# Query, key, silu-gate and merge-gate projections of a two-branch layer as Strassen pairs, with kept operand sums and one branch's products spilled

## The chip, the cores and the metric

One Trainium2 chip, one core. The metric is the device time of one execution in microseconds (us). Before the change three runs gave a median of 2404.2 us (2403.67 to 2405.09). Every product is made in 4-byte numbers split in two parts (below), on TensorE (PE); VectorE is DVE, ScalarE is ACT, GpSimd is POOL, and SyncE (SP) issues the weight loads.

## The reference

Two layers over 512 frames of width 1024. A layer is an RMSNorm, one wide projection, two recurrent branches, a gated merge, a feed-forward block and a gated embedding:

```python
h = rmsnorm(x, norm1_g[i]);  z = h @ w_in[i] + b_in[i]
_, _, mv, mo, mi, mf, rq, rk, rv, rg, gm, gr = split_cols(z)
...                                        # branch A: mLSTM, 4 heads, y_m = sigmoid(mo) * headnorm(hm)
rq4 = rope(rq...);  rk4 = rope(rk...) * (R_DK ** -0.5)
hr = retention_chunkwise(rq4, rk4, rv, log_gamma)          # 4 heads, 256 wide q and k, 512 wide v
y_r = silu(rg) * head_layernorm(hr, r_norm_g[i], R_HEADS)
merged = sigmoid(gm) * (y_m @ w_bm[i]) + sigmoid(gr) * (y_r @ w_br[i])
x = x + merged @ w_out[i]
h2 = rmsnorm(x, norm2_g[i])
x = x + square(relu(h2 @ w_ff1[i] + b_ff1[i])) @ w_ff2[i] + b_ff2[i]
x = x + sigmoid(rmsnorm(x, norm3_g[i]) @ w_pe_gate[i]) * (p[i] @ w_pe[i])
```

## The kernel before, in words

Activations stand transposed, 8 tiles of 128 features by 512 frames. **Each operand is a pair of high and low parts**: `split` (L238) makes the high part by an ACT copy into the rounded type, and the low part by a DVE subtraction (L240). `mm3` (L313) multiplies high by high, high by low and low by high, so one product costs three matmuls. The norm's factor per frame (`n1.b`) is multiplied in after the product, since the projection runs on `x` times the gain (`xa`).

The program is **a list of units** (`unit_list`, L110), in the order in which PE takes them. A `T8` unit is one weight block of 1024 by 128 (512 KB): 24 matmuls of 512 columns into one PSUM bank (`t8`, L318). A `V` unit is a quarter of a value projection, 24 matmuls as well. A `PAIR` unit, used by the second feed-forward product (`ff2`) alone, makes two output tiles over 1024 of the 4096 inner columns by Strassen's scheme in Winograd's form: 7 products of 12 matmuls of 256 columns, 84 in all, in the order P1, (P4 of the pair before), P5, P2, P6, P3, P7. Three PSUM banks serve a pair: P1, P6, P7 and P4 accumulate in bank a, P2 in b, P5 and P3 in c, and after most of the products DVE reads the bank before the next one adds to it. A pair's weights are four blocks and four sums of blocks, in pieces A, B, C (128 by 1024) and D (128 by 512).

Weights flow through **three stages**: `fill_raws` (L276) loads raw pieces on SP's queue into 5 buffers; `prep_next` (L289) splits the next piece, ACT then DVE, into one of 3 buffers (`PIECES`); PE uses it. `ready` (L300) places the split of piece n+2 ahead of unit n's matmuls (`LOOK`), so a split is issued when the buffer of three pieces earlier has been used.

The sums of blocks (t1 to t4) are made in DRAM by POOL: `sum_steps` (L251) copies 1 MB and adds 1 MB with accumulating DMAs, 8 steps for each of the 8 groups of four pairs. `unit` (L304) issues one slot of this list at every third unit; each step waits for the matmul that stood last, as a pace.

A layer's stages, one after the other: 4 mLSTM heads (query and key with a convolution, whose 3 border columns POOL copies at L689; scores, whose diagonal POOL masks at L736; `attend`; output gate `m_out`), with the merge gate A (`gate_tile`, L813) in between, kept in `mA`; retention head 0's query and key (`r_qk`, L767: product times norm, z, at L775, then the rotation at L781 to L783, then a split); the first branch's output product, multiplied into `mA` (L870 to L872); values, scores, `attend` and the gates (`r_out`, L803) of the retention heads; the second branch's product and gate B (L900 to L913); `w_out`; the feed-forward block; the embedding gate. Short-lived tiles come from `tmp`, a ring of 7 tiles of 128 by 512. Cosine and sine lie in tiles of their own. `decay`, `br_spill` and the residual `xr` are loaded on ACT's queue.

An engine takes its instructions in the order in which they stand in its queue; where one waits, all behind it wait.

Of the kernel before, what the change touches and what calls it, by code (L numbers as in the profile page):

```python
# [53 lines left out]
RAWS = 5  # L54
# [40 lines left out]
STEP = 3  # L95


def pair_schedule(n):

    out = []  # L100
    for i in range(n):
        out.append((i, "P1"))
        if i:
            out.append((i - 1, "P4"))
        out += [(i, x) for x in ("P5", "P2", "P6", "P3", "P7")]
    out.append((n - 1, "P4"))
    return out


def unit_list(i):  # L110
# [9 lines left out]

    def mqk(h):
# [9 lines left out]
    def rqk(h):  # L131
        for d in range(2):
            t8("w_in", CRQ + h * 256 + d * P)
        for d in range(2):
            t8("w_in", CRK + h * 256 + d * P)

    def rg(h):
        for d in range(4):
            t8("w_in", CRG + h * 512 + d * P)
# [15 lines left out]
    full("w_in", CGM, 0, 2, 8)  # L155
    mo(3)
    rqk(0)
    full("w_bm")
# [12 lines left out]
    for c in range(8):  # L171
        t8("w_in", CGR + c * P)
        t8("w_br", c * P, 1024)
    full("w_out")
    def pairs(seq):
        for kind, b, p in seq:
            if kind == "f":
                t8("w_ff1", b * 1024 + 256 * p)
                t8("w_ff1", b * 1024 + 256 * p + P)
            else:  # L180
                u.append(("PAIR", i, b, p))
# [9 lines left out]
def build(ctx, tc, ins, out):  # L191
# [27 lines left out]
    br_dram = tc.dram_tile([L, KT, P, T], F32, name="br_spill")  # L219

# [4 lines left out]
    ones = cpool.tile([P, P], F32, name="ones")  # L225
    gp.memset(ones, 1.0)
    ones_r = cpool.tile([P, P], F32R, name="ones_r")
    ve.tensor_copy(ones_r, ones)
# [14 lines left out]
    sums = {(i, b, x): tc.dram_tile([4, P, Q], F32, name=f"s{i}{b}{x}") for i in range(L) for b in range(4) for x in MADE}  # L243

    def block(i, b, x):
        return ins["wpairs"][i, b, GIVEN.index(x)] if x in GIVEN else sums[i, b, x]
# [4 lines left out]
    def sum_steps(i):  # L251

        def copy(b, x):
            return gp.dma_start(flat(block(i, b, x)), flat(block(i, b, MADE[x][0])), max_dma_last_dim=4096)

        def add(b, x):
            return gp.dma_start(flat(block(i, b, x)), flat(block(i, b, MADE[x][1])), accum_op=OP.add,
                                max_dma_last_dim=4096)

        def step(f, b, x):  # L260

            if f:
                tc.add_manual_dep(f(b, x).ins, cur["mm"].ins.name, SYNC, reason="pace of the sums")

        for b in range(4):
            for f, x in ((copy, "t1"), (copy, "t3"), (add, "t1"), (add, "t3"), (copy, "t2"), (None, None), (add, "t2"),
                         (None, None), (copy, "t4"), (None, None), (add, "t4")):
                yield lambda f=f, b=b, x=x: step(f, b, x)
# [5 lines left out]
    at = {"unit": 0, "prep": 0, "load": 0, "whole": 0}  # L274

    def fill_raws(most=RAWS):  # L276
        while at["load"] < len(order) and len(raws) < most:
            n, x = order[at["load"]]
            raws[n, x] = r = wpool.tile([P, UN], F32, name=f"wr{at['load']}", tag="wr", bufs=RAWS)
            if x:  # L280
                _, i, b, p = units[n]
                for k, y in enumerate(PIECE[x]):
                    nc.sync.dma_start(r[:, k * Q:(k + 1) * Q], block(i, b, y)[p])
# [5 lines left out]
    def prep_next():  # L289
# [5 lines left out]
        pl = cur["xw"] if x == "D" else cur["last"] if n >= NU - LAST else wpool  # L295
        out_ = [pl.tile([P, w], F32R, name=f"w{a}{n}_{x}", tag=f"{'d' if x == 'D' else 'w'}{a}") for a in "hl"]
# [7 lines left out]
    def unit(kind):  # L304
        n = at["unit"]
        at["unit"] += 1
        if n % STEP == 0 and "mm" in cur:
            next(cur["steps"], lambda: None)()
# [9 lines left out]
    def t8(act, name):  # L318
# [16 lines left out]
    class Pair:  # L335


        def __init__(self, name, n, act, done):
            self.name, self.n, self.act, self.done = name, n, act, done
            self.bank = {}  # L340

        def product(self, x):
            w, half, j = PRODUCTS[x]
            ready(place[self.n, "A"] + READY[x])
            wh, wl = [a[:, half * Q:(half + 1) * Q] for a in pieces[self.n, w]]
            b = {"P2": "b", "P5": "c", "P3": "c"}.get(x, "a")
            first = x in ("P1", "P2", "P5")
            if first:
                self.bank[b] = ps(f"{self.name}{b}")
            o = self.bank[b][:, 0:S]  # L350
            m = slice(j * S, (j + 1) * S)
            for k in range(4):
                s = slice(k * P, (k + 1) * P)
                h, l = self.act[k]
                f, e = first and k == 0, k == 3
                te.matmul(o, wh[:, s], h[:, m], start=f, stop=False, skip_group_check=True)
                te.matmul(o, wh[:, s], l[:, m], start=False, stop=False, skip_group_check=True)  # L357
                te.matmul(o, wl[:, s], h[:, m], start=False, stop=e, skip_group_check=True)
            self.done(x, o)

    def run_pairs(make):

        n = at["unit"]
        at["unit"] += len(make)
        live = {}
        for i, x in pair_schedule(len(make)):
            if i not in live:
                live[i] = make[i](n + i)
            live[i].product(x)
            if x == "P4":  # L370
# [853 lines left out]
```

## Time and profile before

| | |
|---|---|
| median of 3 runs | 2404.2 us |
| the profiled execution | 2404.53 us |
| its span (first to last instruction) | 2402.8 us |
| granted TensorE clock, mean | 0.996 |
| PE busy, matmuls | 2381.9 us (99%), 12212 |
| DVE busy | 1500.7 us (62%) |
| ACT busy | 1051.8 us (44%) |
| POOL busy | 178.9 us (7%) |
| moved by DMA | 333.72 MB, 139 GB/s |

"Busy" counts from an instruction's start to its end, and matmuls overlap; what one matmul costs PE is the distance between two starts. A group's row gives its count, busy time, mean duration and the idle time of its engine just before it with what ended that. A wait row gives the microseconds an engine stood still, how often and the longest. A DMA row gives the size of one and the median time from issue to landing.

### The profile page before, as it was taken

The numbers are of one execution on the slowest core, as the hardware profiler recorded it, in microseconds if no ns is written. First come the engines' busy times: TensorE is split into PE (matmuls) and PEld (weight loads), VectorE is DVE, ScalarE is ACT, GpSimd is POOL, SyncE is SP. The second block draws the span as 40 slices with busy tenths as digits, with TensorE's granted clock in tenths as the row PEclk, the third lists the DMA queues.
The fourth block names the chain that finished last, engine by engine and source line by source line (L and its number), as shares of the span: only waits on it lengthen the run. The fifth ranks groups of instructions, "written<-read, shape, count | busy, mean of one in ns | idle before, by whom it ended". The sixth has DMA issues, their size and how long they took to land.

```text
span 2402.8 us, 31079 instructions
## 1 busy us (share of the span) xinstructions
PE 2381.9 (99%) x12212; PEld 2036.4 (85%) x12212; DVE 1500.7 (62%) x2276; ACT 1051.8 (44%) x1434; POOL 178.9 (7%) x266
## 2 busy tenths in 40 slices
PE   9999999999999999999999999999999999999997
PEld 8888888888888898899888888888888888998996
DVE  6867536654555576677778665466625556676675
ACT  5746323332333445445557552233323335445453
POOL 3101000000000100000201100000000010000012
PEclk9999999999999999999999999999999999999998
DMA  6433453545365553444444445344454654443451
GB/s 229 134 103 110 146 149 105 150 127 167 113 169 165 151 158 117 141 154 132 147 142 125 127 119 163 118 123 133 122 167 136 175 167 123 154 146 116 140 161 36
DMA packets 114883, 333.72 MB, mean 139 GB/s; under 512 B 11689, under 2 KB 14121, under 8 KB 114737
## 3 DMA queue, kind: packets, MB, share of 16 engines
q1 hardware_dynamic: 87392, 246.66, 31.2%
q0 software_dynamic: 17408, 67.11, 11.8%
q10 hardware_dynamic: 9936, 17.96, 2.4%
q8 instruction: 96, 1.57, 0.3%
q14 instruction: 51, 0.41, 0.1%
HBM read 323.30 MB, written 75.50 MB: 166 GB/s over the span
## 4 chain that ended last, share of the span: by engine, by line
PE 97%; DVE 1%; issue 1%; DMA 1%; POOL 0%; ACT 0%; SPq 0%; POOLq 0%; DVEq 0%; ACTq 0%
PE l0f L314 2%; PE l1f L314 2%; PE l1f L316 2%; PE l1f L315 2%; PE l0f L316 2%; PE l0f L315 2%; PE l1br L315 1%; PE l1br L314 1%; PE l0br L314 1%; PE l0br L316 1%; PE l0br L315 1%; PE l1br L316 1%; PE l0bgm L314 1%; PE l1bgm L314 1%; PE l0pg L314 1%; PE l0pg L315 1%
## 5 line engine op out<-in xcount | busy, mean ns | idle before, releaser
L239 ACT ACTIVATE wh<-wr 128x1024 fp32r<-128x1024 f32 x342 | 362.0, 1059 | 836.2 <-issue 161.7
L240 DVE TENSOR_TENSOR wl<-wr,wh 128x1024 fp32r<-128x1024 f32 x342 | 418.4, 1224 | 220.5 <-ACT wh L239 220.0
L314 PE MATMUL l0f<-l0n2h,wh 128*128 128x512 f32 x256 | 99.8, 390 | 0.0
L314 PE MATMUL l1f<-l1n2h,wh 128*128 128x512 f32 x256 | 99.8, 390 | 0.0
L316 PE MATMUL l1f<-l1n2h,wl 128*128 128x512 f32 x256 | 99.7, 389 | 0.0
L316 PE MATMUL l0f<-l0n2h,wl 128*128 128x512 f32 x256 | 99.7, 389 | 0.0
L315 PE MATMUL l1f<-l1n2l,wh 128*128 128x512 f32 x256 | 99.6, 389 | 0.0
L315 PE MATMUL l0f<-l0n2l,wh 128*128 128x512 f32 x256 | 99.6, 389 | 0.0
L239 ACT ACTIVATE wh_C<-wr 128x1024 fp32r<-128x1024 f32 x32 | 33.9, 1060 | 67.4 <-PE l0f L315 5.6
L316 PEld LDWEIGHTS l0f<-l0n2h,wl 128*128 128x128 f32 x256 | 48.1, 188 | 10.2
L316 PEld LDWEIGHTS l1f<-l1n2h,wl 128*128 128x128 f32 x256 | 48.0, 188 | 10.1
L314 PEld LDWEIGHTS l1f<-l1n2h,wh 128*128 128x128 f32 x256 | 48.1, 188 | 9.8
L315 PEld LDWEIGHTS l1f<-l1n2l,wh 128*128 128x128 f32 x256 | 48.1, 188 | 9.8
L315 PEld LDWEIGHTS l0f<-l0n2l,wh 128*128 128x128 f32 x256 | 48.1, 188 | 9.7
L314 PEld LDWEIGHTS l0f<-l0n2h,wh 128*128 128x128 f32 x256 | 48.1, 188 | 9.7
L240 DVE TENSOR_TENSOR wl_C<-wr,wh_C 128x1024 fp32r<-128x1024 f32 x32 | 39.2, 1226 | 18.3 <-ACT wh_C L239 17.9
L239 ACT ACTIVATE wh_A<-wr 128x1024 fp32r<-128x1024 f32 x32 | 33.8, 1056 | 30.5 <-PE l1f L315 9.8
L240 DVE TENSOR_TENSOR wl_A<-wr,wh_A 128x1024 fp32r<-128x1024 f32 x32 | 40.4, 1264 | 10.3 <-ACT wh_A L239 9.4
L239 ACT ACTIVATE wh_B<-wr 128x1024 fp32r<-128x1024 f32 x32 | 33.7, 1053 | 27.1 <-PE l0o02a L357 1.8
L240 DVE TENSOR_TENSOR wl_B<-wr,wh_B 128x1024 fp32r<-128x1024 f32 x32 | 39.1, 1221 | 7.9 <-ACT wh_B L239 7.9
L239 ACT ACTIVATE wh_D<-wr 128x512 fp32r<-128x512 f32 x32 | 20.1, 628 | 37.1 <-PE l0o01a L357 1.8
L429 POOL TENSOR_TENSOR l1n3sum<-l1n3sum,l1n3sq 128x512 f32<-128x512 f32 x6 | 8.2, 1360 | 331.3 <-ACT l1n3sum L421 306.8
(3709 smaller groups left out, 7545.6 us busy)
## 6 DMA issues: line engine op xcount, KB each, us to landing
wr<-wstream SPq DMA_DIRECT2D x342, 512.0 KB, 3.4
wr<-wpairs SPq DMA_DIRECT2D x96, 256.0 KB, 2.7
s00t<-wpairs POOLq DMA_DIRECT2D x6, 1024.0 KB, 8.9
s01t<-wpairs POOLq DMA_DIRECT2D x6, 1024.0 KB, 8.6
s02t<-wpairs POOLq DMA_DIRECT2D x6, 1024.0 KB, 8.9
s03t<-wpairs POOLq DMA_DIRECT2D x6, 1024.0 KB, 8.5
s10t<-wpairs POOLq DMA_DIRECT2D x6, 1024.0 KB, 9.4
s11t<-wpairs POOLq DMA_DIRECT2D x6, 1024.0 KB, 9.1
```

Source lines behind the costliest of these rows:

```text
L239: ac.activation(hi_ap, src, AF.Copy)
L240: ve.tensor_sub(lo_ap, src, hi_ap.bitcast(F32))
L314: te.matmul(o, sh, mh, start=first, stop=False)
L315: te.matmul(o, sh, ml, start=False, stop=False)
L316: cur["mm"] = te.matmul(o, sl, mh, start=False, stop=last)
L429: gp.tensor_tensor(self.sum, self.sum, sq, OP.add)
```

## The change

- **46 more pairs.** Retention's queries and keys (8 pairs a layer), its silu gates (8), merge gate A's tiles 2 to 7 (3) and gate B (4) become PAIR units; each takes the place of two T8 units. Matmuls of 512 columns go from 8476 to 6260, of 256 columns from 3076 to 6940.
- **A pair's last product is put off.** `run_pair` leaves P4, the bank's reading and the consumer in `later`; `flush` runs them after the next pair's P1, in the middle of the next T8 unit, after the first V unit, ahead of the scores, after `attend`'s first tile or after the first transpose of `back`.
- **A pair's products are put together in two `tmp` tiles**: P1, P5, P6 and P4 are copied out of PSUM by ACT (256 columns), P2, P7 and P3 added by DVE (256 columns). The second tile has the opposite sign, which `scaled` turns.
- **The operand's sums** (`xs_sums`, four times a layer) are made during the mLSTM heads: `x` is loaded again on ACT's queue, scaled by ACT, combined by DVE and split. They are kept in the space of `mA` and in one more tile.
- **Spills.** Gate A's tiles 0 to 3 go to DRAM and come back in the stage of the first branch's product; all 8 of that branch's gated products go to DRAM (`bm_spill`) and come back in gate B's stage. All of these are issued on ACT's queue.
- **The sums of weights** go from 8 groups to 20: 160 steps on POOL instead of 64, the first 20 at every 5/4 units, the others at every 7/4 (`due`).
- **Space.** Raw weight buffers 5 to 4, `tmp` ring 7 to 6, one tag for all weight parts, POOL's descriptor space 2048 to 1024; cosine and sine are loaded on ACT's queue into the convolution's tiles; the value bias uses the ring. The mLSTM heads' row factor is one matmul over 36 rows instead of two over 4 (8 matmuls fewer in all).

The instructions of ACT around the first retention head's query and key, before (`wh` are split weights, `qh` and `kh` the high parts of query and key, `brqu` the rotated query):

```order
L239 ACTIVATE wh_0_2620<-wr_2458 128x1024
L239 ACTIVATE wh_0_2667<-wr_2492 128x1024
L239 ACTIVATE l0r0qh_2576<-l0r0brqu_2651 128x512
L239 ACTIVATE wh_0_2700<-wr_2526 128x1024
L239 ACTIVATE l0r0qh_2578<-l0r0brqu_2658 128x512
L239 ACTIVATE wh_0_2748<-wr_2584 128x1024
L239 ACTIVATE l0r0kh_2580<-l0r0brku_2731 128x512
L239 ACTIVATE wh_0_2780<-wr_2618 128x1024
L239 ACTIVATE l0r0kh_2582<-l0r0brku_2738 128x512
```

and now (`brka`, `brkc` are PSUM banks a and c of the key's pair, `brky` its two tiles, `brqy` the query's):

```order
L258 ACTIVATE wh_C<-wr_2671 128x1024
L417 ACTIVATE l0r0brky_2757<-l0r0brka 128x256
L258 ACTIVATE wh_D<-wr_2692 128x512
L429 ACTIVATE l0r0brqy_2647<-l0r0brqa 128x256
L258 ACTIVATE wh_0_2830<-wr_2725 128x1024
L258 ACTIVATE l0r0qh_2639<-l0r0brqu_2794 128x512
L419 ACTIVATE l0r0brky_2758<-l0r0brkc 128x256
L423 ACTIVATE l0r0brky_2758<-l0r0brka 128x256
L258 ACTIVATE wh_0_2864<-wr_2759 128x1024
L1011 DMA l0gml_2894<-gm_spill 128x512
L258 ACTIVATE l0r0qh_2641<-l0r0brqu_2801 128x512
```

The copies of the query's P4 (L429) and of the key's P5 and P6 (L419, L423) are new; the latter two stand behind the split of the rotated query (`l0r0qh_2639`).

DVE at the same place, before:

```order
L775 TENSOR_TENSOR l0r0brqz_2615<-l0r0brq_2590,l0n1rb 128x512
L240 TENSOR_TENSOR wl_0_2621<-wr_2458,wh_0_2620 128x1024
L775 TENSOR_TENSOR l0r0brqz_2649<-l0r0brq_2624,l0n1rb 128x512
L781 SCALAR_TENSOR_TENSOR l0r0brqu_2651<-l0r0brqz_2615,bc,l0cos 128x512
L782 SCALAR_TENSOR_TENSOR l0r0brqw_2652<-l0r0brqz_2649,bc,l0sin 128x512
L781 SCALAR_TENSOR_TENSOR l0r0brqu_2658<-l0r0brqz_2615,bc,l0sin 128x512
L783 TENSOR_TENSOR l0r0brqu_2651<-l0r0brqu_2651,l0r0brqw_2652 128x512
L782 SCALAR_TENSOR_TENSOR l0r0brqw_2659<-l0r0brqz_2649,bc,l0cos 128x512
L240 TENSOR_TENSOR wl_0_2668<-wr_2492,wh_0_2667 128x1024
L240 TENSOR_TENSOR l0r0ql_2577<-l0r0brqu_2651,l0r0qh_2576 128x512
L783 TENSOR_TENSOR l0r0brqu_2658<-l0r0brqu_2658,l0r0brqw_2659 128x512
```

and now:

```order
L259 TENSOR_TENSOR wl_D<-wr_2692,wh_D 128x512
L439 TENSOR_TENSOR l0r0brqy_2647<-l0r0brqy_2647,l0n1rb 128x512
L851 SCALAR_TENSOR_TENSOR l0r0brqu_2794<-l0r0brqy_2647,bc,l0cos 128x512
L852 SCALAR_TENSOR_TENSOR l0r0brqw_2795<-l0r0brqy_2648,bc,l0sin 128x512
L851 SCALAR_TENSOR_TENSOR l0r0brqu_2801<-l0r0brqy_2647,bc,l0sin 128x512
L853 TENSOR_TENSOR l0r0brqu_2794<-l0r0brqu_2794,l0r0brqw_2795 128x512
L852 SCALAR_TENSOR_TENSOR l0r0brqw_2802<-l0r0brqy_2648,bc,l0cos 128x512
L259 TENSOR_TENSOR wl_0_2831<-wr_2725,wh_0_2830 128x1024
L259 TENSOR_TENSOR l0r0ql_2640<-l0r0brqu_2794,l0r0qh_2639 128x512
L853 TENSOR_TENSOR l0r0brqu_2801<-l0r0brqu_2801,l0r0brqw_2802 128x512
L421 TENSOR_TENSOR l0r0brky_2757<-l0r0brkb,l0r0brky_2757 128x256
L259 TENSOR_TENSOR wl_0_2865<-wr_2759,wh_0_2864 128x1024
```

The rotation of the query now starts after its P4 and stands among the key's products. The key's P2 (L421) is added behind the query's rotation.

POOL in the first mLSTM head of layer 0, before (`s00t` are sums of weights in DRAM, `zp` the convolution's border, `l0m0D` the decay's diagonal):

```order
L689 COPY l0m1q1zp<-l0negb 128x3
L736 AFFINE_SELECT l0m0D_812<-l0m0D_812 128x128
L736 AFFINE_SELECT l0m0D_830<-l0m0D_830 128x128
L257 DMA s00t_91<-wpairs 256x1024
L736 AFFINE_SELECT l0m0D_847<-l0m0D_847 128x128
L736 AFFINE_SELECT l0m0D_863<-l0m0D_863 128x128
L689 COPY l0m1k0zp<-l0negb 128x3
L689 COPY l0m1k1zp<-l0negb 128x3
L689 COPY l0m2q0zp<-l0negb 128x3
```

and now:

```order
L290 DMA s1t_94<-wpairs 256x1024
L761 COPY l0m1q0zp<-l0negb 128x3
L761 COPY l0m1q1zp<-l0negb 128x3
L290 DMA s0t_92<-wpairs 256x1024
L290 DMA s1t_95<-wpairs 256x1024
L807 AFFINE_SELECT l0m0D_862<-l0m0D_862 128x128
L807 AFFINE_SELECT l0m0D_880<-l0m0D_880 128x128
L807 AFFINE_SELECT l0m0D_897<-l0m0D_897 128x128
L290 DMA s0t_93<-s0t_92 256x1024
L807 AFFINE_SELECT l0m0D_913<-l0m0D_913 128x128
L290 DMA s1t_94<-wpairs 256x1024
L761 COPY l0m1k0zp<-l0negb 128x3
```

More steps of the sums stand among the border copies and the masks; the fourth mask now stands behind the step that starts a fourth sum (`s0t_93`).

The core of the diff:

```diff
-STEP = 3
...
+def due(k):
+
+    return 3 + 5 * min(k, 20) // 4 + 7 * max(k - 20, 0) // 4
...
     def rqk(h):
-        for d in range(2):
-            t8("w_in", CRQ + h * 256 + d * P)
-        for d in range(2):
-            t8("w_in", CRK + h * 256 + d * P)
+        for a in range(2):
+            pair(f"rqk{h // 2 * 2}", h % 2 * 2 + a)
...
-    full("w_in", CGM, 0, 2, 8)
+    pair("gm", 1)
     mo(3)
     rqk(0)
-    full("w_bm")
+    for p in range(4):
+        if p > 1:
+            pair("gm", p)
+        full("w_bm", 0, 0, 2 * p, 2 * p + 2)
...
+        first = lambda g: [(g, "t1", 0), (g, "t3", 0), (g, "t1", 1), (g, "t3", 1)]
+        second = lambda g: [(g, "t2", 0), (g, "t2", 1), (g, "t4", 0), (g, "t4", 1)]
+        gs = list(index)
+        out = first(gs[0])
+        for a, b in zip(gs, gs[1:]):
+            for x, y in zip(second(a), first(b)):
+                out += [x, y]
+        return out + second(gs[-1])
...
         for k in range(KT):
             s = slice(k * P, (k + 1) * P)
             mm3(o, wh[:, s], wl[:, s], act[0][k], act[1][k], k == 0, k == KT - 1)
+            if k == 3:
+                flush()
...
+        product("P1")
+        flush()
+        for x in ("P5", "P2", "P6", "P3", "P7"):
+            product(x)
+        later.append(last)
+
+    def pair_tiles(name, act, consume):
+
+        y = [tmp(f"{name}y{d}") for d in range(2)]
+        a, b = slice(0, S), slice(S, T)
+
+        def done(x, o):
+            if x == "P1":
+                ac.activation(y[0][:, b], o, AF.Copy)
+            elif x == "P5":
+                ac.activation(y[1][:, a], o, AF.Copy)
+            elif x == "P2":
+                ve.tensor_tensor(y[0][:, b], o, y[0][:, b], OP.add)
+            elif x == "P6":
+                ac.activation(y[1][:, b], o, AF.Copy)
+            elif x == "P3":
+                ve.tensor_tensor(y[1][:, b], o, y[1][:, b], OP.add)
+            elif x == "P7":
+                ve.tensor_tensor(y[1][:, a], o, y[1][:, a], OP.add)
+            else:
+                ac.activation(y[0][:, a], o, AF.Copy)
+                consume(y)
+
+        run_pair(name, act, done)
+
+    def scaled(d, y, nrm, out_):
+
+        if d:
+            ve.scalar_tensor_tensor(out_, y, -1.0, nrm.b, OP.mult, OP.mult)
+        else:
+            ve.tensor_tensor(out_, y, nrm.b, OP.mult)
...
+                def consume(y):
+                    for d in range(2):
+                        scaled(d, y[d], n1, y[d])
+                    for d in range(2):
+                        u = tmp(f"{nm}{bn}u{d}")
+                        w = tmp(f"{nm}{bn}w{d}")
+                        ve.scalar_tensor_tensor(u, y[0], b[0], trig[d][:, :T], OP.add, OP.mult)
+                        ve.scalar_tensor_tensor(w, y[1], b[1], trig[1 - d][:, :T], OP.add, OP.mult)
+                        ve.tensor_tensor(u, u, w, (OP.subtract, OP.add)[d])
+                        split(u, qk[2 * a][d], qk[2 * a + 1][d])
...
+                def consume(g):
+                    for d in range(2):
+                        scaled(d, g[d], n1, g[d])
+                        ac.activation(g[d], g[d], AF.Silu, bias=bcol(i, "brg", 4 * h + 2 * w + d))
...
+        def xs_sums(k):
...
+            t = [tmp(f"l{i}xsr{k}{a}") for a in range(2)]
+            for a in range(2):
+                nc.scalar.dma_start(t[a], x_src[2 * k + a])
+                ac.activation(t[a], t[a], AF.Copy, scale=n1.col(2 * k + a))
+            u = [tmp(f"l{i}xsu{k}{a}") for a in range(2)]
+            a, b = slice(0, S), slice(S, T)
+            ve.tensor_tensor(u[0][:, a], t[0][:, b], t[0][:, a], OP.subtract)
+            ve.tensor_tensor(u[0][:, b], t[1][:, a], t[0][:, a], OP.subtract)
+            ve.scalar_tensor_tensor(u[1][:, a], u[0][:, b], -1.0, t[0][:, b], OP.mult, OP.subtract)
+            ve.scalar_tensor_tensor(u[1][:, b], u[1][:, a], -1.0, t[1][:, b], OP.mult, OP.subtract)
+            for a in range(2):
+                c = slice(a * T, (a + 1) * T)
+                split(u[a], xs_t[k // 2][:, 2 * (k % 2), c], xs_t[k // 2][:, 2 * (k % 2) + 1, c])
...
         qk = r_qk(0)
-        for c in range(KT):
-            o = t8(ym, f"l{i}bm{c}")
-            ve.tensor_tensor(mA[:, c, :], o, mA[:, c, :], OP.mult)
+        for p in range(4):
+            if p > 1:
+                gm_gates(p)
+            for c in (2 * p, 2 * p + 1):
+                if p < 2:
+                    gm[c] = tmp(f"l{i}gml{c}")
+                    nc.scalar.dma_start(gm[c], gm_dram[i, c])
+                o = t8(ym, f"l{i}bm{c}")
+                g = gm.pop(c)
+                ve.tensor_tensor(g, o, g, OP.mult)
+                nc.scalar.dma_start(bm_dram[i, c], g)
...
-            ve.tensor_tensor(mA[:, c, :], mA[:, c, :], t[:, :T], OP.add)
+            ve.tensor_tensor(t, t, gr.pop(c), OP.mult)
+            ve.tensor_tensor(u, u, t, OP.add)
```

More of the change, by code (lines that the diff above doesn't have):

```diff
@@ L53 @@
 WARM = 20
-RAWS = 5
+NTMP = 6
+RAWS = 4
 PIECES = 3
@@ new lines, in build, with step, next_unit @@
+    steps = sum_steps()
+    made = {g: 0 for g in index}
+    def step():
+        g, x, a = steps[at["step"]]
+        at["step"] += 1
+        made[g] += 1
+        kw = {"accum_op": OP.add} if a else {}
+        dma = gp.dma_start(flat(block(g, x)), flat(block(g, MADE[x][a])), max_dma_last_dim=4096, **kw)
+        tc.add_manual_dep(dma.ins, cur["mm"].ins.name, SYNC, reason="pace of the sums")
+    def next_unit():
+        n = at["unit"]
+        at["unit"] += 1
+        while at["step"] < len(steps) and due(at["step"]) <= n:
+            step()
+        return n
@@ L304, in unit @@
     def unit(kind):
[L305 to L308, printed above, removed]
+        n = next_unit()
         assert units[n][0] == kind, (units[n], kind)
@@ L359, in product @@
[L359 to L370, printed above, removed]
-                del live[i]
-                for w in PIECE:
-                    del pieces[n + i, w]
+                te.matmul(o, wh[:, s], h, start=f, stop=False, skip_group_check=True)
```

347 lines of the change are left out of this document (193 added, 154 removed).

## The prediction, made before the changed kernel had run

> **What bounds the kernel now.** I read the page first: the busy shares, and the chain of work that ended last.
>
> ```profile
> span 2402.8 us, 31079 instructions
> ...
> PE 2381.9 (99%) x12212; PEld 2036.4 (85%) x12212; DVE 1500.7 (62%) x2276; ACT 1051.8 (44%) x1434; POOL 178.9 (7%) x266
> ...
> PE 97%; DVE 1%; issue 1%; DMA 1%; POOL 0%; ACT 0%; SPq 0%; POOLq 0%; DVEq 0%; ACTq 0%
> ```
>
> PE is busy all the time and makes 97% of the chain: only fewer or cheaper matmuls, or new waits, change the time. The next question is what PE waits for today.
>
> ```profile
> PE l1n41ss L438 <- ACT l1n41sq L421: 3.9, 1, 3.9
> PE l1n40rp L455 <- DVE l1n40dh L452: 2.3, 1, 2.3
> ...
> PE l0o33a L356 <- DVE l0x L979: 1.0, 1, 1.0
> PE l0o32a L356 <- DVE l0x L979: 0.7, 1, 0.7
> PE l1o33a L356 <- DVE l1x L979: 0.7, 1, 0.7
> PE l1o32a L356 <- DVE l1x L979: 0.7, 1, 0.7
> ```
>
> Nearly all is at the very end (the last norm). In the branches, where the change works, PE waits for nothing, so nothing is to be gained there but matmul time. The last four rows matter later: they lie in pairs that carry a norm's tiles as additional DVE and ACT work, and each lost 0.7 to 1.0 us to a bank that DVE had not yet read.
>
> A busy PE says nothing of a matmul's price; the distance of starts does.
>
> ```profile
> L314 PE MATMUL l0wo<-l0mh,wh x64: 388/389/395, 759.3 to 802.2; 128*128 128x512 f32 x64
> ...
> L356 PE MATMUL l0o02a<-l0hh,wh_A x4: 280/280/280, 877.4 to 878.5; 128*128 128x256 f32 x4
> ...
> L356 PE MATMUL l0o03a<-l0hh,wh_A x4: 280/280/280, 887.3 to 888.4; 128*128 128x256 f32 x4
> ```
>
> In the first row 64 starts, each the first of three matmuls, lie 42.9 us apart: 42.9 / 63 / 3 = 0.227 us for 512 columns, 24 of them 5.45 us for a T8 unit. The other two are the first product of one feed-forward pair and of the next: 9.9 us for a pair, or 9.9 / 84 = 0.118 us for 256 columns.
>
> **The matmuls.** A pair replaces two T8 units: 10.90 - 9.90 = 1.0 us saved. 46 pairs: **-46 us**. The row factor's 8 matmuls of 512 columns less: 8 x 0.227 = **-1.8 us**. From the profiled execution's 2404.5 us (1.7 us of it outside the span, 0.3 above the median of the runs, so both serve) this leaves 2356.7 us if nothing new waits.
>
> The Trainium skill, TensorE: Matmul & The Clock Gate, section Back-to-back issue gap, speaks against the change: it gives 131 ns a matmul in a sustained stream of 512 columns and 81 ns for 128. My estimate between them for 256 columns is 98 ns; a pair would take 8.2 us, the two tiles 6.3, and 46 pairs would add 89 us. The rows above disagree, 0.227 against 0.118 us: here time goes nearly with the columns.
>
> **What DVE and ACT get in addition.** Their prices:
>
> ```profile
> L239 ACT ACTIVATE wh<-wr 128x1024 fp32r<-128x1024 f32 x342 | 362.0, 1059 | 836.2 <-issue 161.7
> L240 DVE TENSOR_TENSOR wl<-wr,wh 128x1024 fp32r<-128x1024 f32 x342 | 418.4, 1224 | 220.5 <-ACT wh L239 220.0
> ...
> L240 DVE TENSOR_TENSOR wl_D<-wr,wh_D 128x512 fp32r<-128x512 f32 x32 | 22.1, 690 | 2.7
> ...
> L1050 DVE TENSOR_TENSOR l1pgt<-pl,l1n3rb 128x256 f32<-128x256 f32 x8 | 3.4, 425 | 9.5 <-PE pl L316 9.4
> ...
> L1051 ACT ACTIVATE l1pgt<-l1pgt 128x256 f32<-128x256 f32 x8 | 3.3, 413 | 6.1 <-DVE l1pgt L1050 6.1
> ```
>
> ```profile
> L783 DVE TENSOR_TENSOR l0r0brqu<-l0r0brqu,l0r0brqw x2: 685/685/685, 287.9 to 290.9; 128x512 f32<-128x512 f32 x2
> L239 ACT ACTIVATE l0r0qh<-l0r0brqu x2: 634/634/634, 288.6 to 291.6; 128x512 fp32r<-128x512 f32 x2
> ...
> L781 DVE SCALAR_TENSOR_TENSOR l0r0brqu<-l0r0brqz,bc,l0cos x1: 744/744/744, 285.9 to 285.9; 128x512 f32<-128x512 f32 x1
> ```
>
> A pair splits three and a half pieces where two tiles split two: DVE 1.224 + 0.690 = 1.91 us, and three additions at 0.425; ACT 1.059 + 0.634 and four copies at 0.413. For 46 pairs that is 147 us on DVE and 154 on ACT. `xs_sums` brings 4 x 0.425 + 2 x 0.69 = 3.1 us of DVE each, 25 us for eight. DVE comes to about 1673 us, 71% of the span, ACT to about 1230, 52%. In sum neither bounds; in places they may.
>
> *Second pair of two in a row* (a head's key, the second half of a head's gates: 16 places). The copy of P5 stands on ACT behind the consumer of the pair before, and P3 adds into P5's bank. For the query's rotation, from the end of its P4: ACT copy 0.41, `scaled` 0.69, three rotations 0.744 each, the subtraction 0.685, the split's ACT copy 0.634, then P5's copy 0.41: 5.06 us. Meanwhile PE has P5, P2 and P6, 36 x 0.118 = 4.25 us. PE is **0.8 us late**. The four feed-forward pairs with added work lost 0.7 to 1.0 us, so I take 0.85 for each of the 16, the gates too, where the chain has two activations in place of the rotation: **+13.6 us**. Below it is 0, if the chain overlaps better. Above, all DVE work of a key's pair: 3 x 1.224 + 0.69 of splits, 3 x 0.425, 1.43 of `scaled`, 4 x 0.744 + 2 x 0.685 of rotation, 1.37 of its split = 12.8 us against 9.9 on PE: 2.9 us each, 46 us. Behind the waiting copies ACT holds only the next weight splits; PE waits for those.
>
> *First pairs and lone pairs* (30): their P4 comes in the middle of a T8 or V unit, or after P1 of the next pair, with other banks in between; that unit's matmuls hide it. Without this cover they would cost the same 0.85 us, 26 us more. I take 0.
>
> *Around the third and fourth mLSTM heads.* Stages, by windows:
>
> ```profile
> 200.00:274.00 74.00, 74.00 (x369) 62.65 (x368) 44.55 (x91) 35.35 (x57) 7.55 (x10) 1.00 0.42 126
> ...
> 871.00:896.00 25.00, 25.00 (x215) 25.00 (x214) 18.52 (x29) 10.18 (x11) 0.00 (x0) 1.00 0.67 199
> ```
>
> In the first (PE, weight loads, DVE, ACT, POOL; clock, DMA share) DVE has 44.6 of 74 us. Four gate tiles leave it (21.8 us of PE, 4 x 1.91 of DVE), two become a pair (+3.2 of DVE), one `xs_sums` enters: 43.3 us of DVE in 51 of PE, 85%. The weight buffers carry a bunch of some us. I take 1 us a layer, **+2**; from 0 to 5 us a layer.
>
> **What DMA gets.**
>
> ```profile
> q1 hardware_dynamic: 87392, 246.66, 31.2%
> q0 software_dynamic: 17408, 67.11, 11.8%
> q10 hardware_dynamic: 9936, 17.96, 2.4%
> ...
> wr<-wstream SPq DMA_DIRECT2D x342, 512.0 KB, 3.4
> wr<-wpairs SPq DMA_DIRECT2D x96, 256.0 KB, 2.7
> ...
> s10t<-wpairs POOLq DMA_DIRECT2D x6, 1024.0 KB, 9.4
> ```
>
> A step of the sums takes 0.118 x 2402.8 / 64 = 4.43 us of all DMA engines; 160 take 709 us. The weights go from 246.7 to 283 MB (92 T8 pieces of 0.52 MB less, 46 pairs of 1.84 MB more), at 3.04 us a MB 860 us. ACT's queue doubles with the spills and reloads, some 115 us. Together 71% of the span, now 45%. Densest are the first 20 steps, at every 5/4 units of layer 0:
>
> ```profile
> 27.00:185.00 158.00, 158.00 (x752) 131.82 (x752) 122.99 (x219) 91.13 (x141) 20.61 (x42) 0.99 0.45 132
> ```
>
> Eight steps or so lie in these 158 us now, 35 us or 0.22 of the share; twenty would be 89 us, 0.56: 0.45 - 0.22 + 0.56 = 0.79. The feed-forward pairs run at 0.67 without PE waiting for a weight, and a piece is loaded four pieces ahead, 9.9 us in pairs, against a landing of 3.4. So I take **+2 us**, for the heads whose masks and border copies stand on POOL behind a step that awaits an earlier one's landing (9.4 us, two steps being 13.6 us apart). Bounds: 0, and 50 us, worked out under the rivals. The 96 more issues on POOL (7% busy), the reloads on ACT and SP's shorter pieces are hidden by the buffers.
>
> A gain below these zeros is excluded: PE waited for nothing in those stages.
>
> Sum: 2404.5 - 46 - 1.8 + 13.6 + 2 + 2 = **2374 us**.
>
> **The rivals.**
>
> *Nothing new waits* (13%): 2356 to 2364 us. For it: T8 units leave splits far ahead. Against it: the chain of 5.06 us against 4.25.
>
> *DVE and ACT bind in the retention heads* (13%): 16 places at up to 2.9 us instead of 0.85, 2388 to 2399 us. For it: 12.8 us of DVE in a pair of 9.9. Against it: the V and T8 units around them need little DVE (their split 1.22 us in 5.45).
>
> *DMA is late in the first 28 units of layer 0* (12%, **slower than before**). If a step holds the DMA engines not for 4.43 us but for most of its 9.4 us of landing, say 8, twenty take 160 us of the 158, and the other traffic there, 0.45 - 0.22 of 158 us, another 36: 38 us of it do not fit, and the later groups come late by as much, so that PE waits for weights or sums; with half as much again in layer 0's retention heads, some 50 us, 2424 us. It decides from a step of 122 / 20 = 6.1 us on, and is slower than before from about 7.6. For it: landings are twice the 4.43 us. Against it: a landing also holds the time in which weight loads interleave, and those landed in 3.4 us beside the steps. The Trainium skill, DMA: Bandwidth & Descriptors, section Issuing engines are not separate DMA queues, says that transfers from all queues share 16 engines and interleave; the page counts the three queues, 31.2, 11.8 and 2.4%, as shares of the same 16 engines, which agrees.
>
> *The new pairs' matmuls have a fixed price* (3%, slower): a pair ceases to gain at 48 x 0.227 / 84 = 0.130 us a matmul; at 0.135 the 46 pairs lose 20 us against before, 2440 us with the waits. For it: in the window of pairs above the weight loads are busy 25.00 of 25.00 us. Against it: 0.118 in just these pairs. It is also the case in which the change doesn't do what it says; the skill's section above would put it there.
>
> *Within 0.2%*, 4.8 us, about what a measurement of this kernel tells from no change: 7%, the second rival at its upper end with some of the third.
>
> **How the numbers follow.** The forecast, 2364 to 2388 us, has 52%; with the first two rivals faster has 78%, same 7%, slower 15%. The range goes from 2356, no wait at all, to 2404: it leaves out the last two rivals and a part of the same, a little under 2 in 10.
>
> **What would show it.** Starts of consecutive pairs of retention's keys and gates 9.9 us apart plus a wait of 0.5 to 1.5 us in P3 on ACT's copy of P5 (right); the same for the first pairs of each head (the cover fails); wait rows of PE on weights or on a piece's split (DMA or DVE); DMA share in the first 185 us near 0.8, landings of the steps near 10 us; DVE at about 71%. I am wrong if PE's waits exceed 40 us in sum, or if the new pairs' starts lie over 10.9 us apart without a wait.

## The result and the profile after

The changed kernel takes **2423.7 us** (median of 4 runs, 2422.8 to 2431.1) against 2404.6 before (median of 4, 2403.7 to 2407.1): a ratio of 1.0085, interval 1.0063 to 1.0106. I had forecast 2374. The loss is clear of the noise. The page:

```profile
span 2421.1 us, 35877 instructions
...
PE 2365.9 (98%) x13860; PEld 2094.6 (87%) x13860; DVE 1646.8 (68%) x2553; ACT 1203.1 (50%) x1745; POOL 257.9 (11%) x366
...
q1 hardware_dynamic: 119952, 281.82, 34.9%
q0 software_dynamic: 43520, 167.78, 29.4%
q10 hardware_dynamic: 19728, 35.79, 4.2%
```

PE is busy 16 us less than before, but the span is 18 us longer. The totals came out about as foreseen: DVE 68% of the span (71 foreseen), the weights' queue 282 MB (283), the steps of the sums on q0 29.4% of the DMA engines (30). The loss is not in these totals. PE's waits show where it is:

```profile
PE l1m2ot L619 <- DVE l1m2num L613: 11.4, 1, 11.4
PE l0m2ot L619 <- DVE l0m2num L613: 7.4, 1, 7.4
PE l0m0ot L619 <- DVE l0m0num L613: 6.4, 1, 6.4
...
PE l1m0ot L619 <- DVE l1m0num L613: 3.2, 1, 3.2
...
PE l1r3brkc L394 <- ACT l1r3brky L419: 0.8, 1, 0.8
```

The four large ones are the transposes (`ot`) of the first (`m0`) and third (`m2`) mLSTM head in both layers, which wait for DVE to finish the head's norm (`num`). The last row is a key's pair waiting for ACT's copy of P5.

A wait row does not count matmuls that are merely slow. So I added up, over the traces, the distances between successive starts of matmuls: each at its price before (0.2268 us for 512 columns, 0.1179 for 256), what exceeds it by over 0.2 us as a wait, the rest as slowness. In us:

| | before | change |
|---|---|---|
| matmuls at the prices of before | 2364.7 | 2317.7 |
| waits in the mLSTM heads | 1.3 | 41.3 |
| waits in the keys' pairs | 0 | 5.0 |
| other waits (start, feed-forward, end) | 14.6 | 14.3 |
| the new pairs' matmuls slower than 0.1179 | 0 | 13.5 |
| other slowness | 13.2 | 20.4 |
| sum, first to last start | 2393.8 | 2412.2 |

Fewer matmuls brought 47.0 us. The mLSTM heads took 40 of it, the new pairs' own price 13.5, the keys 5.0, other slowness 7.2. The four large waits alone are 29.0 of the 41.3 us. Behind each of them the matmuls are slow: the transposes of `l0m2ot` took 421 ns instead of 272. The granted clock of the change is 0.50 from 119.5 to 125.3 us, from 235.0 to 241.4 and from 1430.2 to 1436.0, right behind three of these waits, and 1.00 from 60 to 110 us; in before it is 1.00 from 190 to 235 us, without such a drop. Matmuls at the halved clock are about 12 us of the loss: 8 of them exceed their price by over 0.2 us and so are counted in the row of the heads' waits, 4 in the rows of slowness.

**The third head.** ACT and then DVE in the changed kernel, from the second sum in this head on (start, duration, what it does, the idle time before it and what ended that):

```profile
203.93 0.34 ACTq L936 DMA_DIRECT2D l0xsr<-xT  x1
...
206.25 0.33 ACTq L936 DMA_DIRECT2D l0xsr<-xT  x1
...
209.30 0.72 ACT L937 ACTIVATE l0xsr<-l0xsr,bc 128x512 f32<-128x512 f32 x1 [0.89 <-DMA l0xsr<-xT]
211.84 0.72 ACT L937 ACTIVATE l0xsr<-l0xsr,bc 128x512 f32<-128x512 f32 x1 [1.82 <-DMA l0xsr<-xT]
```

```profile
210.06 0.42 DVE L940 TENSOR_TENSOR l0xsu<-l0xsr 128x256 f32<-128x256 f32 x1 [0.38 <-ACT l0xsr L937]
212.60 0.43 DVE L941 TENSOR_TENSOR l0xsu<-l0xsr,l0xsr 128x256 f32<-128x256 f32 x1 [2.12 <-ACT l0xsr L937]
...
234.34 1.38 DVE L613 TENSOR_SCALAR l0m2num<-l0m2num,l0m2mv,l0m2hv 128x256 f32<-128x256 f32 x4
```

`x` is loaded again at 203.9 and 206.3 and lands over 5 us later. ACT stands for it, DVE stands for ACT, and behind them stand the next head's convolution and this head's statistics. From 212.6 to 233.0 DVE does not rest; then it stands 1.2 us for a factor from POOL, as it did in before, and makes `num` from 234.3. PE, whose unit ahead had its last start at 227.1, can start the transposes at 234.9. What room there had been is in the trace of before:

```profile
L546 PE MATMUL l0m2ot<-ident,l0m2num x8: 270/272/273, 220.6 to 221.4; 128*128 128x128 f32 x8
...
L540 DVE TENSOR_SCALAR l0m2num<-l0m2num,l0m2mv,l0m2hv x4: 406/408/411, 215.9 to 216.9; 128x256 f32<-128x256 f32 x4
```

`num` was done at 217.3, the transposes began at 220.6: **3.3 us of room**, into which the change put a sum of 3.1 us of DVE and 2.5 us of waits for ACT inside it.

**The first head.** POOL in the changed kernel:

```profile
106.48 0.91 POOL L290 DMA_DIRECT2D s0t<-wpairs  x1 [4.50 <-DVE l0m0mv L608]
107.05 0.53 POOL L761 COPY l0m2q1zp<-l0negb 128x3 f32<-128x3 f32 x1
116.58 0.89 POOL L290 DMA_DIRECT2D s1t<-wpairs  x1 [9.00 <-issue]
117.17 1.37 POOL L828 TENSOR_TENSOR l0m0hv<-l0m0hv,nhalf 128x4 f32<-128x4 f32 x1
```

The norm factor `l0m0hv` stands behind a step of the sums that stood still for 9.0 us with no semaphore to explain it ("issue"). By the trace the step of 106.48 landed at 116.3, 0.3 us before this one began. DVE waited 8.3 us for this factor.

### The profile page after: what moved, and what is told of

Same layout as the page of the kernel before. It is cut to its first block, busy times and chain, and to the rows that moved or that the text cites. A ratio compares the mean times of both kernels' runs of the same rounds, so it can differ in the third digit from the quotient of the medians.

```text
span 2421.1 us, 35877 instructions
## 1 busy us (share of the span) xinstructions
PE 2365.9 (98%) x13860; PEld 2094.6 (87%) x13860; DVE 1646.8 (68%) x2553; ACT 1203.1 (50%) x1745; POOL 257.9 (11%) x366
## 3 DMA queue, kind: packets, MB, share of 16 engines
q0 software_dynamic: 43520, 167.78, 29.4%
## 4 chain that ended last, share of the span: by engine, by line
PE 44%; DVE 3%; ACT 1%; issue 1%; DMA 1%; POOL 0%; POOLq 0%; DVEq 0%; ACTq 0%
PE l1f L345 2%; PE l1f L346 2%; PE l1f L347 2%; PE l1br L347 1%; PE l1br L345 1%; PE l1br L346 1%; PE l1wo L345 1%; PE l1bm L347 1%; PE l1wo L347 1%; PE l1wo L346 1%; PE l1bm L345 1%; PE l1bm L346 1%; DMA wr<-s11t 0%; DVE wl L259 0%; PE l1pg L345 0%
## 5 line engine op out<-in xcount | busy, mean ns | idle before, releaser
L258 ACT ACTIVATE wh<-wr 128x1024 fp32r<-128x1024 f32 x250 | 264.1, 1058 | 394.3 <-issue 61.8
L259 DVE TENSOR_TENSOR wl<-wr,wh 128x1024 fp32r<-128x1024 f32 x250 | 307.1, 1229 | 159.0 <-ACT wh L258 158.4
L258 ACT ACTIVATE wh_C<-wr 128x1024 fp32r<-128x1024 f32 x78 | 82.5, 1058 | 131.2 <-DMA wr<-wstream 8.8
L259 DVE TENSOR_TENSOR wl_B<-wr,wh_B 128x1024 fp32r<-128x1024 f32 x78 | 95.4, 1223 | 45.4 <-ACT wh_B L258 45.3
L258 ACT ACTIVATE wh_B<-wr 128x1024 fp32r<-128x1024 f32 x78 | 82.3, 1055 | 75.4 <-PE l0r1vp L563 3.6
L258 ACT ACTIVATE wh_A<-wr 128x1024 fp32r<-128x1024 f32 x78 | 82.4, 1057 | 71.6 <-PE l1f L346 11.3
L259 DVE TENSOR_TENSOR wl_A<-wr,wh_A 128x1024 fp32r<-128x1024 f32 x78 | 96.6, 1238 | 23.6 <-ACT wh_A L258 23.6
L258 ACT ACTIVATE wh_D<-wr 128x512 fp32r<-128x512 f32 x78 | 49.1, 629 | 123.5 <-DMA wr<-s11t 10.4
L259 DVE TENSOR_TENSOR wl_C<-wr,wh_C 128x1024 fp32r<-128x1024 f32 x78 | 95.2, 1221 | 22.1 <-ACT wh_C L258 21.3
L259 DVE TENSOR_TENSOR wl_D<-wr,wh_D 128x512 fp32r<-128x512 f32 x78 | 53.6, 688 | 80.7 <-ACT wh_D L258 73.8
```

The costliest lines, as they stand in the source:

```text
L258: ac.activation(hi_ap, src, AF.Copy)
L259: ve.tensor_sub(lo_ap, src, hi_ap.bitcast(F32))
```

## The experiments

Times are medians; the kernel before had medians of 2404.7 to 2405.7 beside them. Several of these kernels spread over 4 to 14 us, with a granted clock that goes from 0.991 to 0.997 along with it, so I read the traces first and differences of a few us in the medians second. A trace is one execution: those of 2, 3 and 9 are 4 to 6 us faster than their medians, those of 8 and 10 are 11 and 5 us slower.

**1. Longer rows in the sum steps.**

```diff
-        dma = gp.dma_start(flat(block(g, x)), flat(block(g, MADE[x][a])), max_dma_last_dim=4096, **kw)
+        dma = gp.dma_start(flat(block(g, x)), flat(block(g, MADE[x][a])), max_dma_last_dim=8192, **kw)
```

> The sum steps' DMAs are made of rows of 8 KB instead of 4 KB, so each needs half as many descriptors; nothing else is changed. Theory (a step stands on POOL until an earlier one has freed descriptor space, and the norm factor of the first mLSTM head stands behind it): the wait of PE for the first head's transposes in layer 0, 6.4 us, is gone or under 2 us, and the time falls by 5 to 10 us to about 2416; layer 1's 3.2 us stay. Rival (the step waits for its pace or for the landing of the copy before it): no change, 2422 to 2426 us.

Measured: 2414.4 us (ratio 1.0036, 1.0024 to 1.0049), 9 us better than the change. POOL at the same place:

```profile
102.30 0.84 POOL L290 DMA_DIRECT2D s0t<-wpairs  x1 [0.49 <-PE l0m0a L347]
...
107.74 0.82 POOL L290 DMA_DIRECT2D s1t<-wpairs  x1 [3.20 <-PE l0m0o L347]
110.23 1.04 POOL L828 TENSOR_TENSOR l0m0hv<-l0m0hv,nhalf 128x4 f32<-128x4 f32 x1 [1.67 <-DVE l0m0hv L827]
```

The step now waits for its pace alone and the factor is not late; PE's 6.4 us are gone from the wait rows, layer 1's 3.2 are still there, and the third head's wait in layer 0 is 9.4 instead of 7.4. The step of 107.74 begins while the one of 102.30 is still under way (it lands at 110.5), which the stalled step of the change did not. Fewer descriptors in each step take the stall away, so the step had most likely waited for room for them; the change halved that room, and no run gave it back.

**2. No operand sums**, and **3. sums without the reload.** In 2 `xs_sums` returns at once and `xs(k)` gives parts of `xa`; in 3:

```diff
-            t = [tmp(f"l{i}xsr{k}{a}") for a in range(2)]
-            for a in range(2):
-                nc.scalar.dma_start(t[a], x_src[2 * k + a])
-                ac.activation(t[a], t[a], AF.Copy, scale=n1.col(2 * k + a))
+            t = [xa[0][2 * k + a].bitcast(F32) for a in range(2)]
```

> The operand's sums are left out altogether (no second load of x, no scaling, no combining, no splits); the pairs read parts of the old operand in their place, so PE's work is the same and the result is not the reference's. Theory (the sums in the third mLSTM head make DVE and ACT late and PE waits 7.4 and 11.4 us for that head's transposes): both waits are gone and the time falls by 22 to 32 us, to 2392 to 2402. Rival (sum steps on POOL and DMA traffic cause the waits in the heads): a gain of 6 us at most, 2418 to 2424.

> The operand's sums are made from the rounded high parts that are in SBUF already, instead of x loaded again and scaled; DVE's work and the splits stay, the loads, their waits on ACT and eight times two ACT scalings go (the result lacks the low parts' share). If the waiting for the reload is what counts: nearly as fast as without any sums, 2395 to 2405. If DVE's added work counts: less than a third of that gain, 2413 to 2420.

Measured: 2396.5 us (0.9947 to 0.9973 of before) and 2402.1 us (0.9971 to 0.9994). PE's waits without sums, then without the reload alone:

```profile
PE l1m0ot L619 <- DVE l1m0num L613: 3.2, 1, 3.2
PE l1n40rp L522 <- DVE l1n40dh L519: 2.3, 1, 2.3
PE l1m2ot L619 <- DVE l1m2num L613: 1.6, 1, 1.6
```

```profile
PE l1m2ot L619 <- DVE l1m2num L613: 2.7, 1, 2.7
PE l1m0ot L619 <- DVE l1m0num L613: 2.4, 1, 2.4
```

By the addition above, the waits in the mLSTM heads fall from 41.3 to 12.0 and 15.3 us. So nearly all that the sums cost is the reload with its waits and scalings on ACT; DVE's work for them costs about 3 us by the traces, 6 by the medians. In 3 the two tiles of the reload also leave the `tmp` ring. Experiment 7, which keeps them there and adds DVE work, has 18.4 us of waits in the heads against 33.3 in experiment 1, so the ring is not needed to explain the gain.

**4. No steps of the sums of weights.** `block` gives a given block for each made one, and `step` issues nothing.

> The 160 steps on POOL are left out; the pairs load given blocks in place of the sums, so loads, splits and matmuls are the same and the result is not the reference's. Theory (steps matter only where POOL's masks and norm factors stand behind them, in the first head): the waits in the first heads go, 9.6 us, the waits in the third heads stay at over 14 us, 2405 to 2414. Rival (contention for DMA engines makes weights and reloads late, and slows the new matmuls): the waits in the third heads go too and 256 columns take 0.118 us as in the feed-forward pairs, 2375 to 2395.

Measured: 2396.4 us (0.9946 to 0.9976). Both guesses are half right: the first heads' waits go, the third heads' fall to 4.3 us each, 8.6 together, not to "over 14" and not to nothing, and the time falls between the two ranges:

```profile
PE l0m2ot L616 <- DVE l0m2num L610: 4.3, 1, 4.3
PE l1m2ot L616 <- DVE l1m2num L610: 4.3, 1, 4.3
```

The steps act on the third head at least in part through the reload, whose landing is the last line of the view of that tile, in the change and here (minimum, median, maximum):

```profile
DMA to landing us min/median/max: 3.4/5.2/6.2
```

```profile
DMA to landing us min/median/max: 2.6/3.1/5.3
```

The steps are POOL's and the reload ACT's, on queues of their own. The Trainium skill, DMA: Bandwidth & Descriptors, section Issuing engines are not separate DMA queues, says that such transfers interleave on the same 16 engines; the landings agree. The new pairs' matmuls stay at 0.120 us: the traffic is not what makes them slower. No row of any of these traces has PE waiting for a weight's landing, and in the change and here its waits for a weight's split are under 1 us each.

**5. One part undone: silu gates as T8 units.**

```diff
-        for a in range(2):
-            pair(f"rg{h // 2 * 2}", h % 2 * 2 + a)
+        for d in range(4):
+            t8("w_in", CRG + h * 512 + d * P)
```

> One part undone: retention's silu gates are T8 units again (16 pairs fewer, 32 T8 units more; the steps that make their sums still run). If a pair saves 1.0 us, as I had it: 16 us slower than the change, 2440. If it saves what the starts of the changed kernel give, 84 x 0.120 = 10.1 and some 0.2 us of hitches against 10.9: 9 us slower, 2433. If the gates' pairs cost more than they save: 2424 or less.

Measured: 2419.5 us (1.0040 to 1.0070), 4 us *faster* than the change, the last of the three cases by its time. By the trace it is the second: at the old prices 32 T8 units for 16 pairs cost 15.7 us, and 5.2 of slowness in new pairs go, 10.5 us net or 0.66 us a pair. But the waits in the mLSTM heads, whose program is unchanged, were 29.7 us instead of 41.3. In layer 0, ahead of any of these gates, the difference is 2.9 us. In layer 1 it is 8.6 us, behind layer 0's gates, where the steps fall at other moments: 103 of the 160 had been issued before that layer's heads, 99 in the change. Such stalls seem to hang on when steps and landings fall, and a median alone would have misled.

**6. Activations 64 bytes wider** (on top of 2).

```diff
-            hi.append(pl.tile([P, T], F32R, name=f"{name}h{k}", tag="ah", bufs=KT))
+            hi.append(pl.tile([P, T + 16], F32R, name=f"{name}h{k}", tag="ah", bufs=KT)[:, :T])
...
```

> As the kernel without the operand's sums, but each tile of the normed activations is 64 bytes wider, so that the tiles no longer start at multiples of 2 KB. If the new pairs' 0.120 us a matmul (0.118 in the feed-forward pairs, whose tiles are 7 KB wide) comes of where the moving operand lies: 256 columns go to 0.118 and the time falls by 5 to 8 us against that kernel. If not: 0.120 stays, no change within 4 us.

Measured: 2410.3 us, 14 slower than experiment 2. The 256-column matmuls do what the expectation said, and its sum fails. A product of a new pair and the embedding gate's T8 units, in the change and here (durations, minimum, median, maximum; a 256-column matmul lasts 280 ns at starts 0.118 us apart and 283 at 0.120):

```profile
L394 PE MATMUL l0gr1b<-l0n1h,wh_B x4: 283/283/283, 706.2 to 707.3; 128*128 128x256 f32 x4
...
L345 PE MATMUL l0pg<-l0n3h,wh x64: 387/389/486, 1157.1 to 1202.9; 128*128 128x512 f32 x64
```

```profile
L394 PE MATMUL l0gr1b<-l0n1h,wh_B x4: 280/281/282, 690.8 to 691.9; 128*128 128x256 f32 x4
...
L345 PE MATMUL l0pg<-l0n3h,wh x64: 388/394/476, 1145.6 to 1192.2; 128*128 128x512 f32 x64
```

256 columns get faster (slowness in new pairs 13.8 to 8.7 us), 512 columns slower (7.1 to 28.7).

**7. Sums from SBUF** (with the rows of 1): the two parts are added instead of loading `x`.

```diff
-                nc.scalar.dma_start(t[a], x_src[2 * k + a])
-                ac.activation(t[a], t[a], AF.Copy, scale=n1.col(2 * k + a))
+                ve.tensor_tensor(t[a], xa[0][2 * k + a].bitcast(F32), xa[1][2 * k + a].bitcast(F32), OP.add)
```

> The operand's sums take high part plus low part from SBUF (one DVE addition of 512 columns for each of two tiles) in place of the load and ACT's scaling, and the sum steps have rows of 8 KB; the result is the reference's. Theory (the reload's waiting and the step ahead of the norm factor made most of the loss): both earlier gains add up, 2392 to 2400 us, waits for the transposes of the mLSTM heads under 8 us in sum. Rival (the two are the same DVE lateness seen twice, and 1.4 us more of DVE in each of the sums gives back what is gained): 2402 to 2410.

Measured: 2399.7 us, 0.9982 of before (0.9973 to 0.9991). The time lies in the range of the theory, but of the two earlier gains, 9 and 22 us, only 24 together come, and 10 us of waits for transposes are left (5.0, 2.6 and 2.5), 2 more than I allowed.

**8. The last two sums in the stage of the first branch's product**, with that stage's first four units ahead of the first query and key, and gate A's tiles 2 and 3 as T8 units:

```diff
-    pair("gm", 1)
+    full("w_in", CGM, 0, 2, 4)
...
-        xs_sums(2)
         qk = m_qk(3)
...
                 nc.scalar.dma_start(bm_dram[i, c], g)
+                if c < 2:
+                    xs_sums(2 + c)
```

> As the version with sums from SBUF, but gate A's tiles 2 and 3 are T8 units again, and the last two of the operand's sums stand in the stage of the first branch's product, whose first four units now come ahead of the first retention head's query and key. Theory (the third and fourth mLSTM heads have no room on DVE): the waits for m2's transposes and in m3's attend are gone, 2 to 6 us faster than that version in spite of two pairs fewer, 2388 to 2396. Rival (no DVE limit is left there once the reload is gone): slower by the two pairs, 1 to 2 us.

Measured: 2406.3 us (2403.6 to 2417.6), 1.0011 of before (1.0000 to 1.0021). No gain against before is shown. The trace is of the slowest of ten executions, 11 us above the median, so it shows where this order can wait and not what the median waits for. The heads' waits fall to 3.4 us, but others come in their place:

```profile
PE l1f L346 <- ACT l1n2h L475: 7.1, 1, 7.1
PE l0r0brqb L397 <- DVE wl_B L260: 4.6, 1, 4.6
...
PE l0bgm2c L395 <- ACT l0bgm2y L420: 2.2, 1, 2.2
PE l1bgm2c L395 <- ACT l1bgm2y L420: 2.2, 1, 2.2
```

Directly behind the sums stand pairs, whose splits and copies are late now; `l1f` waits at the start of the feed-forward block, behind the residual's load from DRAM, which landed 8.1 us after its issue (median; 4.5 in the change). The theory was right on the heads, and the forecast was wrong.

**9. The sums one place later and a slower pace** (on top of 7): gate A's tiles 2 and 3 as T8 units, sum 2 after `m_out(2)`, sum 3 after `m_attend(3)`, and

```diff
-    return 3 + 5 * min(k, 20) // 4 + 7 * max(k - 20, 0) // 4
+    return 3 + 3 * min(k, 20) // 2 + 7 * max(k - 20, 0) // 4
```

> As the version with sums from SBUF, with gate A's tiles 2 and 3 as T8 units, the third and fourth of the operand's sums one place later each, and the first 20 steps at every 3/2 units. Theory (the third mLSTM head's waits come of the sums standing ahead of its statistics on DVE): 7.5 us of waits for m2's transposes fall under 2, two pairs fewer cost 1.2 us, 2392 to 2397. Rival (the waits move to the next head or to the first pairs, as they did when the sums stood in the product stage): 2400 or more.

Measured: **2389.9 us** (2385.4 to 2394.9), 0.9936 of before (0.9924 to 0.9949): faster than both kernels, with two pairs fewer in all, and 2 us below the range of its theory. The waits in the mLSTM heads are 5.3 us in sum, and the row for the third heads' transposes is gone. The order, the tiles and the pace were changed together; which of them did how much is not shown.

**10, 11. The kept sums 64 bytes further in their tiles**, on top of 7 and of 9:

```diff
-                xs_t[k // 2] = pl.tile([P, 4, 4 * S], F32R, name=f"l{i}xs{k}", tag=tg)
+                xs_t[k // 2] = pl.tile([P, 16 * S + 16], F32R, name=f"l{i}xs{k}", tag=tg)[:, 16:].rearrange("p (a b) -> p a b", a=4)
```

> As the version with sums from SBUF, but the kept sums lie 64 bytes further in their tiles, so that their parts no longer start at multiples of 1 KB; only the new pairs read them, for 4 of their 7 products. If the place of the moving operand sets 0.120 or 0.118 us: 46 x 48 matmuls get 0.002 us shorter, 4 to 5 us less, 2394 to 2396. If it was something else in the kernel with wider tiles: no change, 2398 to 2401.

> The last version with the kept sums shifted by 64 bytes as well. If the two gains are independent: 4 to 5 us less than it, 2388 to 2393. If not: no change against it.

Measured: 2411.8 and 2400.9 us, 12 and 11 us slower than without the shift. New pairs win 4 us in each, but T8 units that never read a kept sum get slower (the first branch's product; the change, with which experiment 7 agrees in this row, then experiment 10). 64 bytes more in one tile can move what is laid behind it; the addresses themselves are not on record.

```profile
L345 PE MATMUL l0bm<-l0ymh,wh 128*128 128x512 f32 x64 | 25.0, 390 | 0.0
```

```profile
L345 PE MATMUL l0bm<-l0ymh,wh 128*128 128x512 f32 x64 | 25.4, 396 | 0.0
```

So the lie of the tiles sets both prices, but my reading that each new pair's own operand decides is not shown.

**12. Neither sums nor steps.**

> Neither the operand's sums nor the steps on POOL (pairs read old parts and given blocks instead; the result is not the reference's). If the two overlap in the same wait (the reload lands late because of the steps): not 27 + 27 us better than the change but about 38, 2384 to 2388: what is left against 2357 is the key pairs' waits (6), the matmuls at 0.120 and their hitches (16). If they add up: 2370 or less.

Measured: 2379.3 us (0.9876 to 0.9906), 44 better than the change; they overlap, though less than I had thought. The mLSTM heads have 4.0 us of waits left, the keys 5.0, the new pairs 13.4 of slowness. With the 2356.7 us of the prediction's matmuls this makes 2379.1: little else is left.

## Why the prediction was wrong

- **The matmuls** (-47.8): right as a count, 47.0 at the old prices. The price of 0.118 us was taken from the feed-forward pairs and failed for the new ones: 0.120 and some hitches, +13.5 us, so that a pair saves 0.7 us and not 1.0. The trace of before had the sign: its last 256-column matmuls (`pl`), on halves of 512-column tiles as in the new pairs, last 283 ns and not 280.

```profile
L314 PE MATMUL pl<-l1n3h,wh x64: 278/283/363, 2359.8 to 2386.2; 128*128 128x256 f32 x64
```

- **Second pair of two in a row** (+13.6): right for the keys in mechanism, the wait on P5's copy is 0.8 us in the first and fourth heads, 0.4 in the third, none in the second, 5.0 us by the addition. The gates' eight places cost nothing, so the term was 8.6 us too large.
- **First and lone pairs** (0): right but for gate A's pair in the heads, 1.2 us above the old price in each layer where the other two pairs of that gate have 0.3.
- **Around the third and fourth mLSTM heads** (+2, at most 5 a layer): **this step failed**, together with the word that the reloads on ACT "are hidden by the buffers". I took a mean over 74 us, 85% of DVE, where the chain of one head decides: 3.3 us of room in before, and a load on which ACT, DVE and then PE stand one behind the other. Of the 40 us in the heads, 26 go when the reload goes (3) and 29 when the sums go (2). I also left out that ACT, in its order, cannot pass a scaling that awaits a DMA, and I had no term for the clock behind a wait, some 12 us. My window began at 200 us. The sum that made the third head late stands on DVE ahead of an instruction that ran at 192.6 in before, so the window missed it, and the four gate tiles that I took out of the window ran from 226 to 262, behind the transposes of 220.6. In the stretch that counts DVE was already at 25.15 of 31 us in before:

```profile
190.00:221.00 31.00, 31.00 (x154) 26.29 (x153) 25.15 (x50) 18.25 (x28) 3.11 (x4) 1.00 0.23 76
```

- **What DMA gets** (+2, at most 50): shares right, 0.78 in the first window against 0.79 (with 18 steps in it instead of twenty, and 6 in before instead of eight). The price was 8 us for POOL's queue in the first head (1), and the steps' share in the reload's landing; both together 23 us of waits (4). I had weighed the landings against the pace of the steps, but not the room for descriptors, which the change itself had halved.
- **The slower rival** gave 2424 us, but by another way: full DMA engines making weights late. PE never waited on a weight's landing in the change, so its number is a coincidence (38 us and half as much again are 57, not 50, besides). That the steps cost time was right: without them the change is 27 us faster (4). The second rival, DVE and ACT binding in the retention heads, did not happen: DVE and ACT bound, but in the mLSTM heads.
- **Range and chances**: my sign of being wrong, waits of PE over 40 us in sum, came true with 60.6 by the addition. I gave slower 15% although three unknown costs (a load that engines wait for, POOL's queue, a price from another stage) all point to the slow side.

What stays open: how the waits in the heads split between reload and steps is not fixed, since either removal shrinks both; and layer 1's 3.2 us in the first head stay without the sums and with longer rows (3.2) and fall to 0.6 without the steps, but also in experiment 5, where the steps only fall at other moments; by which way they act is not shown, and POOL's masks behind a step are one.

## What to carry to other kernels

Work moved under a busy engine has to be weighed against the room of the one chain that passes there (when its result was ready, when it was used), not against the mean load of the stage: here 3.3 us decided, with DVE at 81% in that stretch before. A load whose user sits in an in-order queue costs its landing for all that stands behind; if the data, or its parts, lie in SBUF already, one addition is cheaper. When one engine both issues bulk DMAs and does small steps on the critical chain, room for descriptors is most likely part of the budget.

## What the runs showed of the hardware that I had not expected

- The place of tiles in SBUF moves matmul times by 1 to 2%, with opposite signs: with tiles of the activations 64 bytes wider, 256 columns go from 283 to 281 ns, 512 columns from 389 to 394; with the kept sums 64 bytes further, new pairs win 4 us and the first branch's product goes from 390 to 396. What in the place decides was not found.
- Behind a wait of 7.4 us the transposes ran at 421 ns instead of 272, and the granted clock was 0.50 from 235.0 to 241.4 us, over 6 us after PE had begun again. The traces of 9 and 12, which have no such long wait in the heads, have no such stretch there. A wait costs more than itself.
- A DMA of 1 MB in rows of 4 KB on POOL's queue could stand for 9 us without a semaphore and began 0.3 us after an earlier one had landed; in rows of 8 KB it did not stand.
